# FFN-in products of eleven pairs of steps by seven block products for eight, with two of four weight sums made by transfers that add in place

## The chip, the cores and the metric

One core of one Trainium2 chip runs the kernel. The metric is the device time of one execution in microseconds (us); the median of 3 runs before the change is 1057.72 us (1057.66 to 1057.72). One more execution was recorded by the hardware profiler. The engines are named as in the profile: PE (TensorE, the matmuls), PEld (its weight loads), DVE (VectorE), ACT (ScalarE), POOL (GpSimd), SP (SyncE, which only issues transfers).

## The reference

A decoder trunk of two layers on 256 tokens of width 1024, in float32. Each layer is four blocks, each with a norm ahead and a norm behind it; the FFN blocks, with D_FF = 2816, are what the change touches:

```
def swiglu(x, w_in, w_out):
    gate, up = jnp.split(x @ w_in, 2, axis=-1)
    return (jax.nn.silu(gate) * up) @ w_out
...
        h = swiglu(rms_norm(x, g[0]), w_ffn_in[layer, 0], w_ffn_out[layer, 0])
        x = x + 0.5 * rms_norm(h, g[1])
        h = mixer(rms_norm(x, g[2]))      # layer 0: mLSTM, layer 1: differential attention
        x = x + rms_norm(h, g[3])
        h = swiglu(rms_norm(x, g[4]), w_ffn_in[layer, 1], w_ffn_out[layer, 1])
        x = x + 0.5 * rms_norm(h, g[5])
        x = x + rms_norm((p[layer] @ w_ple) * sigmoid(rms_norm(x, g[6]) @ w_gate), g[7])
```

(The body of a layer is given in outline.) So there are four FFNs, two in each layer; the keys and values that the attention reads are projected once, between the layers.

## The kernel before, in words

Every float32 product of the large layers is three products of split numbers. A number is split into a high half (rounded to the format that TensorE takes at full rate) and a low half (the rest); `mm3` adds hi x hi, hi x lo and lo x hi into one PSUM bank. All weights stream from HBM once, as tiles of 1 MB (128 x 2048), through `weight`: SP loads the tile into a slot `wraw`, ScalarE copies it into `whi` (this rounds it), VectorE writes `wlo` = raw - high. There are 3 slots of raw weights and 5 each of `whi` and `wlo`.

The hidden width of an FFN is cut into 11 steps (`NJ`) of 256 columns, the tokens into two tiles `t` of 128. The function `ffn` has for a step j:

- `stage_in(j, t)`: the FFN-in block. Two weight tiles (the two halves of the width of x), 512 columns each: 256 of gate and 256 of up. `in_block` issues 24 matmuls of 128x512 into a PSUM bank `accI` (8 pieces of x, three products each). ScalarE then makes `sg` = silu(gate), VectorE `h` = up x `sg`, TensorE transposes `h` by two matmuls into the bank `tr`, and the transposed `h` is split into `hh` and `hl`.
- `stage_out(j, t)`: the FFN-out block, one weight tile and 12 matmuls for each token tile into `accO`, which sums over the 11 steps.

The loop runs j from 2 on: both `stage_in` of step j, then both `stage_out` of step j - 1. Steps 0, 1 and 10 are written apart, with the norm at the end (`end`: `post`, then `epilogue`, which makes the next block's transposed input).

The order of instructions is not that of this code. Every call goes to a recorder (`Notes`), which keeps the operations with their dependences and a cost for each. A planner (`play`) then puts them in order for each engine as a list scheduler does: by these costs, urgent ones first, the slots of a ring (such as `wraw`) given out in turn as their last users end. Weight loads and splits are recorded as not urgent. The program is issued in that order, so all instructions have one line in the profile, L363 (L371 after the change), and only the names of tiles tell them apart. A DMA queue's instruction waits in that order too: before the change all transfers but a few at the start are issued by SP.

Of the kernel before, what the change touches and what calls it, by code (L numbers as in the profile page):

```python
# [16 lines left out]
P = 128  # L17
D = 1024
# [13 lines left out]
ATT = 8  # L32

# [15 lines left out]
class Notes:  # L49
# [150 lines left out]
    def cost(self, o, outs, ins):  # L200
# [20 lines left out]
        elif o.eng == "vector":  # L221
# [16 lines left out]
    def play(self, margin):  # L238
# [53 lines left out]
        while len(order) < n:  # L292
# [29 lines left out]
            if e == "sync":  # L322
# [20 lines left out]
            for u in o.users:  # L343
                u.left -= 1
                if u.after[o]:
                    u.ready = max(u.ready, o.end if u.eng != e or e == "sync" else clock[e])
# [19 lines left out]
def trunk(nc, a):  # L366
# [9 lines left out]
    def acc_in():  # L376
        return PT("accI", 512)

    def trp():
        return PT("tr", 512)  # L380
# [21 lines left out]

    def weight(src, n=1, m=1, between=None):
        raw = T([P, 2048], "wraw", 3)
        hi = T([P, 2048], "whi", 5, F32R)
        lo = T([P, 2048], "wlo", 5, F32R)
# [56 lines left out]
    mask_a = T([P, 384], "mask_a", 1)  # L465
    nc.gpsimd.memset(mask_a, 0.0)
    for c0 in (0, 256):
        nc.gpsimd.affine_select(
            out=mask_a[:, c0:c0 + P], in_=mask_a[:, c0:c0 + P], compare_op=ALU.is_ge, fill=BIG,
            base=0, pattern=[[1, P]], channel_multiplier=-1,  # L470
        )

# [41 lines left out]
    def post(t, srcs, gbc, coef):  # L514
        hg = T([P, D], "hg", 3)
# [7 lines left out]
    def new_xt():  # L523
        return T([P, KD, P], "xh", 3, F32R), T([P, KD, P], "xl", 3, F32R)


    def transpose4(src, q):
        pt = trp()
# [15 lines left out]
    def gained(xt, pv, gi, q, into=None):  # L544
# [3 lines left out]
        split(xt[0][:, c, :], xt[1][:, c, :], xg)  # L548

# [11 lines left out]
    def pre(gi, rs, kept=None, raws=None):  # L561
        def go(t):
            xt = new_xt()
            for b in (kept, raws):
                if b is not None:
                    b.append(T([P, KD, P], "mix", 6))
            for q in (0, 4):
                pv = transpose4(x[t], q)
                gained(xt, pv, gi, q, kept and kept[t])
# [8 lines left out]
    def ffn(l, f, xts, rs, epilogue, first=None):  # L578
# [3 lines left out]
        gbc = []  # L582

        def stage_in(j, t):
            if j not in wi:
                wi[j] = in_weights(a["ffn_in"][l, f, j], m=2 if j < 2 or j == NJ - 1 else 1)
            pi = acc_in()
            in_block(pi, xts[t], wi[j])
            sg = T([P, 256], "sg", 3)
            h = T([P, 256], "h", 2)  # L590
            nc.scalar.activation(sg, pi[:, :256], AF.Silu, scale=rs[t])
            nc.vector.scalar_tensor_tensor(h, pi[:, 256:], rs[t], sg, op0=ALU.mult, op1=ALU.mult)
            hh = T([P, 2, P], "hh", 5, F32R)
            hl = T([P, 2, P], "hl", 5, F32R)

# [4 lines left out]
            hT[j, t] = hh, hl  # L600

# [13 lines left out]

        steps = [(0, 0), (0, 1), (1, 0), (1, 1)] if first else [(0, 0), (1, 0), (0, 1), (1, 1)]
# [5 lines left out]
        for j in range(2, NJ - 1):  # L622
            for t in range(NT):
                stage_in(j, t)
            stage_out(j - 1, 0)
            if j < NJ - 2:
                stage_out(j - 1, 1)
        j = NJ - 1
        stage_in(j, 0)
        stage_out(j - 1, 0)  # L630
        stage_out(j - 2, 1)
# [3 lines left out]
        stage_out(j - 1, 1)  # L635
# [8 lines left out]
    def ple(l, xts, rs, epilogue):  # L644
# [3 lines left out]
        php = T([P, 2, 2, S], "whi", 5, F32R)  # L648
# [12 lines left out]
        for t in range(NT):  # L661
            eg = T([P, D], "hg", 3)
            hg = T([P, D], "hg", 3)
# [47 lines left out]
    def mlstm(l, xts, rs, raws, epilogue):  # L711
        qkT = [T([P, HA, S], "mix", 6) for _ in range(2)]
# [8 lines left out]
        sel = T([P, HA, P], "cst", 1)  # L721
        nc.gpsimd.memset(sel, 1.0)
        nc.gpsimd.affine_select(
            out=sel, in_=sel, compare_op=ALU.is_equal, fill=0.0,
            base=0, pattern=[[-1, HA], [0, P]], channel_multiplier=1,
        )
        ones = T([P, S], "sg", 3)
# [463 lines left out]
```

## Time and profile before

| | before |
|---|---|
| median of 3 runs | 1057.72 us |
| the profiled execution | 1057.92 us |
| its span in the trace | 1056.2 us |
| granted TensorE clock, mean | 0.999 |
| PE busy | 1043.5 us (99%) |
| DVE busy | 627.6 us (59%) |
| ACT busy | 546.8 us (52%) |
| POOL busy | 53.8 us (5%) |
| moved by DMA | 191.84 MB, mean 182 GB/s |

The busy times are sums over the whole span, and a matmul's recorded time overlaps that of its neighbours, since matmuls are pipelined: the matmuls named `accI` have a mean duration of 0.39 us, while a run of them proceeds in steps of 0.2271 us. A group's row gives line, engine, operation, the tile written and the tiles read with their shape, then the busy time and the mean of one in ns, then the idle time just before such instructions and what ended it. DVE, ACT and DMA have their load unevenly: high in the FFNs, lower around the mixers.

### The profile page before, as it was taken

What the parts mean: (1) busy time and instruction counts of PE and PEld (TensorE: products, weight loads), DVE (VectorE), ACT (ScalarE), POOL (GpSimd) and SP (SyncE); (2) the same over time, 40 slices, a digit from 0 to 9 for tenths busy, and PEclk for the clock granted to TensorE, in tenths of its full rate; (3) what the DMA queues carried; (4) which work ended last, traced back from release to release, by engine and by line L of the source; (5) the groups of instructions that cost most, each with busy time, mean ns of one, the idle gap of its engine ahead of it and who ended that gap; (6) DMA issues with size and microseconds to landing.
All of it is one profiled execution on the core that took longest, in us unless ns stands there. A gap on an engine that the chain in (4) does not pass through costs nothing.

```text
span 1056.2 us, 12324 instructions
## 1 busy us (share of the span) xinstructions
PE 1043.5 (99%) x4884; PEld 854.5 (81%) x4884; DVE 627.6 (59%) x716; ACT 546.8 (52%) x774; POOL 53.8 (5%) x89
## 2 busy tenths in 40 slices
PE   8999999999999999999999999999999999999997
PEld 6888888887888888888888888888878888888886
DVE  6754453765666454555887454545885855454475
ACT  6644343655556444345776344444676654444363
POOL 1000000100010000000120000000101100000010
PEclk9999999999999999999999999999999999999999
DMA  9854544454256554542647645543435465454521
GB/s 323 307 208 165 210 177 165 180 199 156 87 198 230 177 199 163 205 176 95 219 173 265 224 166 193 198 161 120 179 134 186 150 239 189 170 199 160 199 80 40
DMA packets 29731, 191.84 MB, mean 182 GB/s; under 512 B 3689, under 2 KB 4073, under 8 KB 7657
## 3 DMA queue, kind: packets, MB, share of 16 engines
q1 hardware_dynamic: 29672, 191.06, 51.0%
q8 instruction: 38, 0.62, 0.2%
q14 instruction: 21, 0.16, 0.0%
HBM read 189.99 MB, written 1.05 MB: 181 GB/s over the span
## 4 chain that ended last, share of the span: by engine, by line
PE 91%; DVE 3%; DMA 3%; ACT 1%; SPq 1%; issue 0%; POOL 0%; DVEq 0%; POOLq 0%; ACTq 0%
PE accI L363 59%; PE accO L363 28%; PE tr L363 5%; DMA wraw<-in_ffn_in 1%; DMA wg<-in_mlstm_gates 1%; ACT att L363 1%; DVE att L363 1%; SPq L363 1%; DMA wraw<-in_w_kv 0%; DVE sm L363 0%; POOL sm L363 0%; DVE xl_2r L363 0%; DVE wlo_3r L363 0%; DVE wlo_0r L363 0%; DVE wlo_1r L363 0%
## 5 line engine op out<-in xcount | busy, mean ns | idle before, releaser
L363 ACT ACTIVATE sg<-accI,sm 128x256 f32<-128x256 f32 x88 | 41.7, 474 | 168.6 <-PE accI L363 168.4
L363 DVE SCALAR_TENSOR_TENSOR h<-accI,sm,sg 128x256 f32<-128x256 f32 x88 | 42.4, 481 | 81.8 <-ACT sg L363 81.5
L363 ACT ACTIVATE whi_1r<-wraw 128x1024 fp32r<-128x1024 f32 (+2 forms) x51 | 69.2, 1375 | 30.8 <-PE accO L363 18.1
L363 ACT ACTIVATE whi_3r<-wraw 128x2048 fp32r<-128x2048 f32 (+1 forms) x46 | 68.6, 1505 | 31.1 <-PE accO L363 16.3
L363 ACT ACTIVATE whi_0r<-wraw 128x2048 fp32r<-128x2048 f32 (+2 forms) x47 | 69.1, 1476 | 28.7 <-PE accO L363 14.7
L363 ACT ACTIVATE whi_4r<-wraw 128x1024 fp32r<-128x1024 f32 (+1 forms) x50 | 68.8, 1398 | 26.0 <-PE accO L363 16.0
L363 ACT ACTIVATE whi_2r<-wraw 128x1024 fp32r<-128x1024 f32 (+1 forms) x46 | 67.1, 1467 | 23.7 <-PE accO L363 14.8
L363 POOL TENSOR_SCALAR sm<-sm 128x1 f32<-128x1 f32 x32 | 22.4, 698 | 703.4 <-ACT waste L363 703.4
L363 DVE TENSOR_TENSOR wlo_3r<-wraw,whi_3r 128x2048 fp32r<-128x2048 f32 (+1 forms) x21 | 37.2, 1781 | 27.0 <-ACT whi_3r L363 27.0
L363 DVE TENSOR_TENSOR wlo_1r<-wraw,whi_2r 128x2048 fp32r<-128x2048 f32 (+1 forms) x22 | 39.6, 1805 | 22.2 <-ACT whi_2r L363 22.0
L363 DVE TENSOR_TENSOR wlo_3r<-wraw,whi_4r 128x1024 fp32r<-128x1024 f32 (+1 forms) x27 | 42.3, 1576 | 17.0 <-ACT whi_4r L363 17.0
L363 DVE TENSOR_TENSOR wlo_4r<-wraw,whi_0r 128x2048 fp32r<-128x2048 f32 (+1 forms) x22 | 39.4, 1804 | 21.3 <-ACT whi_0r L363 21.3
L363 DVE TENSOR_TENSOR wlo_2r<-wraw,whi_3r 128x2048 fp32r<-128x2048 f32 (+1 forms) x23 | 41.7, 1825 | 17.3 <-ACT whi_3r L363 17.3
L363 DVE TENSOR_TENSOR wlo_0r<-wraw,whi_0r 128x2048 fp32r<-128x2048 f32 (+2 forms) x23 | 39.8, 1734 | 20.1 <-ACT whi_0r L363 20.0
L363 DVE TENSOR_TENSOR wlo_1r<-wraw,whi_1r 128x2048 fp32r<-128x2048 f32 (+2 forms) x25 | 39.9, 1605 | 17.3 <-ACT whi_1r L363 17.3
L363 DVE TENSOR_TENSOR wlo_0r<-wraw,whi_1r 128x1024 fp32r<-128x1024 f32 (+1 forms) x24 | 39.9, 1665 | 16.1 <-ACT whi_1r L363 16.1
L363 DVE TENSOR_TENSOR wlo_4r<-wraw,whi_4r 128x2048 fp32r<-128x2048 f32 (+1 forms) x21 | 37.3, 1782 | 18.1 <-ACT whi_4r L363 17.8
L363 DVE TENSOR_TENSOR wlo_2r<-wraw,whi_2r 128x1024 fp32r<-128x1024 f32 (+1 forms) x22 | 37.3, 1706 | 16.8 <-ACT whi_2r L363 16.8
L363 PE MATMUL accI<-whi_0r,xh_0r 128*128 128x512 f32 x92 | 36.1, 396 | 0.8 <-ACT whi_0r L363 0.8
L363 PE MATMUL accI<-wlo_0r,xh_0r 128*128 128x512 f32 x92 | 36.0, 394 | 0.5 <-DVE wlo_0r L363 0.5
L363 PE MATMUL accI<-wlo_1r,xh_0r 128*128 128x512 f32 x92 | 36.3, 395 | 0.0
L363 PE MATMUL accI<-whi_3r,xh_0r 128*128 128x512 f32 x92 | 36.2, 393 | 0.0
(439 smaller groups left out, 2824.1 us busy)
## 6 DMA issues: line engine op xcount, KB each, us to landing
wraw<-in_ffn_in SPq DMA_DIRECT2D x86, 1024.0 KB, 4.8
wraw<-in_ffn_out SPq DMA_DIRECT2D x44, 1024.0 KB, 4.8
wraw<-in_mlstm_in SPq DMA_DIRECT2D x12, 1024.0 KB, 4.8
wraw<-in_ple_gate SPq DMA_DIRECT2D x8, 1024.0 KB, 4.8
wraw<-in_w_kv SPq DMA_DIRECT2D x8, 1024.0 KB, 4.8
gbc<-in_norm_g SPq DMA_DIRECT2D x8, 512.0 KB, 6.1
wraw<-in_mlstm_out SPq DMA_DIRECT2D x4, 1024.0 KB, 4.7
wraw<-in_diff_q SPq DMA_DIRECT2D x4, 1024.0 KB, 4.7
```

Source lines behind the costliest of these rows:

```text
L363: getattr(getattr(self.nc, eng), name)(*args, **kw)
```

## The change

In each FFN some pairs of neighbouring steps (j, j + 1) are taken together by a new function, `stage_pair`. `PAIRS` names the first steps: 5 and 8 in the first FFN, 2, 5 and 8 in each of the other three, eleven pairs in all. For a pair the product is seen as 2 x 2 blocks: two token tiles by two halves of x's width, times two halves of the width by two steps. The scheme used is Strassen's in the form with seven products (`times`, 12 matmuls each) in place of eight. What comes with it:

- four combined forms of x (`forms`, once in an FFN: sums and differences of the quarters a11, a12, a21, a22, each split again), kept for all pairs of that FFN;
- seven split weights in place of four: the blocks b11, b21, b22 as loaded, and four sums. Two of these (`t3`, `u1`) are made by transfers: SP loads one block into a slot, and GpSimd's queue issues a second transfer of the other block into the same slot with `accum_op=ALU.add`. The other two (`wt2`, `wt4`) are made by VectorE in place in the slot of b11 or b21;
- seven sums of results of 128x512 on VectorE (`total`), and one copy out of PSUM on ScalarE (`p1`). They lie in the ring `att`, from which `hidden` (the second half of the old `stage_in`) reads.

A pair has seven weight transfers in place of four: five loads by SP, into five slots, and two adding transfers into two of the same slots.

Rings change size: `wraw` 3 to 7 slots, `xh` and `xl` 3 to 4, `accI` in PSUM 2 to 3 banks, `tr` 2 to 1, `hh` and `hl` 5 to 3, `hg` and `sg` 3 to 2. The long-lived tiles `mix` of the mixers are now halves of `wraw` slots (function `pair`), so that fewer of the seven are free while they live; five are free through the FFN that opens layer 1. A few constants of the mixers are smaller or lie elsewhere. The planner counts a GpSimd transfer as 1100 ns of issue and a landing at 200 bytes per ns, against 400 for SP's.

```diff
+NRAW = 7
+NPART = 5
+NX = 4
+NH = 3
+PAIRS = ((5, 8), (2, 5, 8), (2, 5, 8), (2, 5, 8))
...
+        elif o.name == "dma_start" and o.eng == "gpsimd":
+            o.dur, o.lat = 1100, math.prod(c for s, c in outs[0].ap) * 4 / 200.0
...
-        return PT("accI", 512)
+        return PT("accI", 512, 3)
     def trp():
-        return PT("tr", 512)
+        return PT("tr", 512, 1)
...
+    def pair(*shape):
+        b = T([P, 2, *shape], "wraw", NRAW)
+        return [b[:, i] for i in range(2)]
...
+                pv = transpose4(x[t], q, acc_in() if q else None)
+                xg = gained(xt, pv, gi, q, kept and kept[t])
+                if xfs is not None:
+                    xfs.append(xg)
...
+            hidden(j, t, pi)
+        def forms():
+            a11, a12, a21, a22 = xfs
+            s1 = T([P, 4, P], "att", ATT)
+            f1, f2 = new_xt(), new_xt()
+            nc.is_urgent = False
+            for out, x0, x1, op, f_, q in (
+                    (s1, a21, a22, ALU.subtract, f1, 0), (a21, a11, a21, ALU.subtract, f2, 0),
+                    (a11, s1, a11, ALU.subtract, f1, 4), (a12, a12, a11, ALU.add, f2, 4)):
+                nc.vector.tensor_tensor(out, x0, x1, op=op)
+                c = slice(q, q + 4)
+                split(f_[0][:, c, :], f_[1][:, c, :], out)
+            nc.is_urgent = True
+            return [(f[0][:, c, :], f[1][:, c, :]) for f in (f1, f2) for c in (slice(0, 4), slice(4, 8))]
+        def stage_pair(j, j2):
+            if not xf:
+                xf.extend(forms())
+            s1, s2, s3, n4 = xf
+            def load(src, plus=None):
+                raw = T([P, 2048], "wraw", NRAW)
+                nc.sync.dma_start(raw, src)
+                if plus is not None:
+                    nc.gpsimd.dma_start(raw, plus, accum_op=ALU.add)
+                return raw
+            def parts(raw):
+                p_ = part()
+                split(*p_, raw)
+                return p_
+            def add(out, v0, v1):
+                nc.vector.tensor_tensor(out, v0, v1, op=ALU.add)
+                return parts(out)
+            nc.is_urgent = False
+            b11 = load(win[j, 0])
+            t3 = load(win[j2, 0], win[j2, 1])
+            u1 = load(win[j, 0], win[j2, 0])
+            w11 = parts(b11)
+            wt2 = add(b11, b11, t3)
+            b21 = load(win[j, 1])
+            w21 = parts(b21)
+            wu1 = parts(u1)
+            wt3 = parts(t3)
+            b22 = load(win[j2, 1])
+            w22 = parts(b22)
+            wt4 = add(b21, b21, b11)
+            nc.is_urgent = True
+            def times(x_, w):
+                acc_ = acc_in()
+                for kk in range(4):
+                    c = slice(kk * 512, (kk + 1) * 512)
+                    mm3([acc_], x_[0][:, kk, :], x_[1][:, kk, :], [w[0][:, c]], [w[1][:, c]], kk == 0, kk == 3)
+                return acc_
+            def quarter(t, q):
+                return xts[t][0][:, q:q + 4, :], xts[t][1][:, q:q + 4, :]
+            def total(v0, v1, op, out=None):
+                if out is None:
+                    out = piece()
+                nc.vector.tensor_tensor(out, v0, v1, op=op)
+                return out
+            m1 = times(quarter(0, 0), w11)
+            p1 = piece()
+            nc.scalar.activation(p1, m1, AF.Copy)
+            u2 = total(times(s2, wt2), p1, ALU.add)
+            hidden(j, 0, total(times(quarter(0, 4), w21), p1, ALU.add, p1))
+            z = total(times(s1, wu1), u2, ALU.subtract)
+            m3 = times(s3, wt3)
+            total(m3, u2, ALU.add, u2)
+            hidden(j2, 1, total(z, m3, ALU.subtract))
+            hidden(j2, 0, total(times(n4, w22), z, ALU.add, z))
+            hidden(j, 1, total(times(quarter(1, 4), wt4), u2, ALU.add, u2))
...
+        last = (1,)
+        j = 2
+        while j < NJ - 1:
+            item = (j, j + 1) if j in PAIRS[2 * l + f] else (j,)
+            if len(item) == 2:
+                stage_pair(*item)
+            else:
+                for t in range(NT):
+                    stage_in(j, t)
+            j += len(item)
+            for i in last:
+                stage_out(i, 0)
+            if j < NJ - 1:
+                for i in last:
+                    stage_out(i, 1)
+                left = ()
+            else:
+                left = last
+            last = item
...
+    xfs = [xT[t][:, c, :] for t in range(NT) for c in (slice(0, 4), slice(4, 8))]
+    xts = ffn(0, 0, xts, rs, xfs, pre(1, rq, kept), first)
+    rs, xfs = [], []
+    xts = mlstm(0, xts, rq, kept, pre(2, rs, xfs=xfs))
     rq = []
-    xts = ffn(0, 1, xts, rs, pre(3, rq))
+    xts = ffn(0, 1, xts, rs, xfs, pre(3, rq))
```

How the rows move. In the rows below `wraw_71` to `wraw_77` are slots of raw weights (71 to 73 before), `whi_0r` to `whi_4r` and `wlo_0r` to `wlo_4r` the five split buffers each, `accI_92` and up PSUM banks, `att_100` and up the ring that holds the forms of x and the results, `hl_0r` and up the low half of the transposed `h`.

VectorE in the middle of the second FFN, before:

```order
L363 TENSOR_TENSOR wlo_4r<-wraw_73,whi_4r 128x2048
L363 SCALAR_TENSOR_TENSOR h_113<-accI_94,sm_9_184,sg_126 128x256
L363 TENSOR_TENSOR wlo_0r<-wraw_71,whi_0r 128x2048
L363 TENSOR_TENSOR hl_3r<-tr_100,hh_3r 128x256
L363 TENSOR_TENSOR wlo_1r<-wraw_72,whi_1r 128x2048
L363 SCALAR_TENSOR_TENSOR h_114<-accI_93,sm_5_180,sg_125 128x256
L363 TENSOR_TENSOR hl_0r<-tr_99,hh_0r 128x256
```

The same engine in a pair of that FFN, after:

```order
L371 TENSOR_TENSOR wraw_73<-wraw_73,wraw_72 128x2048
L371 SCALAR_TENSOR_TENSOR h_109<-accI_93,sm_9_172,sg_116 128x256
L371 TENSOR_TENSOR hl_1r<-tr_99,hh_1r 128x256
L371 TENSOR_TENSOR wlo_4r<-wraw_71,whi_4r 128x2048
L371 TENSOR_TENSOR hl_2r<-tr_99,hh_2r 128x256
L371 TENSOR_TENSOR wlo_3r<-wraw_73,whi_3r 128x2048
L371 TENSOR_TENSOR hl_1r<-tr_99,hh_1r 128x256
L371 TENSOR_TENSOR wraw_71<-wraw_71,wraw_73 128x2048
L371 TENSOR_TENSOR wlo_0r<-wraw_74,whi_0r 128x2048
L371 TENSOR_TENSOR wlo_1r<-wraw_72,whi_1r 128x2048
L371 TENSOR_TENSOR att_105<-accI_92,att_103 128x512
```

Where splits of weights alternated with the work on `h`, two weight sums (wraw from wraw) and the first sum of results stand among them, and a split now waits behind a sum; the first row waits for the adding transfer into `wraw_72`.

VectorE behind step 1 of the second FFN, before (the first splits of steps 2 and 3):

```order
L363 SCALAR_TENSOR_TENSOR h_113<-accI_94,sm_5_180,sg_127 128x256
L363 TENSOR_TENSOR hl_2r<-tr_100,hh_2r 128x256
L363 TENSOR_TENSOR wlo_4r<-wraw_71,whi_4r 128x2048
L363 SCALAR_TENSOR_TENSOR h_114<-accI_93,sm_9_184,sg_126 128x256
L363 TENSOR_TENSOR wlo_0r<-wraw_72,whi_0r 128x2048
L363 TENSOR_TENSOR hl_0r<-tr_99,hh_0r 128x256
```

And after, where the first pair follows:

```order
L371 TENSOR_TENSOR att_103<-att_105,att_107 128x512
L371 TENSOR_TENSOR att_105<-att_104,att_105 128x512
L371 TENSOR_TENSOR hl_0r<-tr_99,hh_0r 128x256
L371 TENSOR_TENSOR att_104<-att_103,att_104 128x512
L371 TENSOR_TENSOR xl_0r<-att_103,xh_0r 128x512
L371 TENSOR_TENSOR xl_1r<-att_105,xh_1r 128x512
L371 TENSOR_TENSOR att_100<-att_100,att_104 128x512
L371 SCALAR_TENSOR_TENSOR h_108<-accI_92,sm_9_172,sg_117 128x256
L371 TENSOR_TENSOR wlo_0r<-wraw_73,whi_0r 128x2048
L371 TENSOR_TENSOR hl_1r<-tr_99,hh_1r 128x256
```

The four forms of x (att from att) and their splits (`xl_0r`, `xl_1r`) have come in ahead of the splits of weights.

VectorE at the second pair of the third FFN, after, from the last read of slot `wraw_75` to the sum that needs the weight that was loaded and added there:

```order
L371 TENSOR_TENSOR wlo_4r<-wraw_75,whi_0r 128x2048
L371 TENSOR_TENSOR hl_1r<-tr_99,hh_1r 128x256
L371 SCALAR_TENSOR_TENSOR h_109<-att_107,sm_1_164,sg_116 128x256
L371 TENSOR_TENSOR wlo_0r<-wraw_73,whi_1r 128x2048
L371 TENSOR_TENSOR hl_2r<-tr_99,hh_2r 128x256
L371 TENSOR_TENSOR wlo_1r<-wraw_72,whi_2r 128x2048
L371 TENSOR_TENSOR wlo_2r<-wraw_74,whi_3r 128x2048
L371 TENSOR_TENSOR wlo_3r<-wraw_77,whi_4r 128x2048
L371 SCALAR_TENSOR_TENSOR h_108<-accI_92,sm_10_173,sg_117 128x256
L371 TENSOR_TENSOR wraw_77<-wraw_77,wraw_75 128x2048
```

Between the two reads of `wraw_75` stand four splits of weights, two `h` and two `hl`; in that time a load by SP and an adding transfer have to land in it.

GpSimd's queue ahead of the second FFN (the norms' small operations `sm`), before and after:

```order
L363 TENSOR_TENSOR sm_15_152<-sm_14_151,mhalf_136 128x4
L363 TENSOR_TENSOR sm_2_139<-sm_1_138,mhalf_136 128x4
L363 TENSOR_SCALAR sm_1_176<-sm_4_141 128x1
L363 TENSOR_TENSOR sm_3_178<-sm_1_176,mhalf_136 128x1
L363 TENSOR_SCALAR sm_2_177<-sm_5_142 128x1
```

```order
L371 TENSOR_TENSOR sm_2_127<-sm_1_126,mhalf_124 128x4
L371 DMA wraw_75<-in_ffn_in 128x2048
L371 DMA wraw_76<-in_ffn_in 128x2048
L371 TENSOR_SCALAR sm_1_164<-sm_4_129 128x1
L371 TENSOR_TENSOR sm_3_166<-sm_1_164,mhalf_124 128x1
```

Two adding transfers of the second FFN's first pair have moved in ahead of the norm that closes the mLSTM block.

More of the change, by code (lines that the diff above doesn't have):

```diff
@@ L345, in play @@
                 if u.after[o]:
-                    u.ready = max(u.ready, o.end if u.eng != e or e == "sync" else clock[e])
+                    u.ready = max(u.ready, o.end if u.eng != e or o.name == "dma_start" else clock[e])
                     if u.eng != e:
@@ L634, in ffn @@
         stage_in(j, 1)
-        stage_out(j - 1, 1)
+        for i in last:
+            stage_out(i, 1)
         stage_out(j, 1)
@@ L711, in mlstm @@
     def mlstm(l, xts, rs, raws, epilogue):
-        qkT = [T([P, HA, S], "mix", 6) for _ in range(2)]
+        qkT = pair(HA, S)
         qT, kT = qkT
@@ L891, in shared_k @@
     def shared_k(xts, rs):
-        kT = [T([P, 4, S], "mix", 6) for _ in range(2)]
+        kT = pair(4, S)
         ws = [in_weights(a["w_kv"][b], m=2) for b in range(2)]
@@ L924, in diff_attn @@
         lam_init = 0.8 - 0.6 * math.exp(-0.3 * l)
-        qT = [T([P, 4, S], "mix", 6) for _ in range(2)]
+        qT = pair(4, S)
         ws = [in_weights(a["diff_q"][b]) for b in range(2)]
```

138 lines of the change are left out of this document (64 added, 74 removed).

## The prediction

> **What bounds the kernel now.** I read the page's busy line first, then TensorE's own waits, then the chain of waits, then busy time by stage. The columns of the busy line are engine, us, share and instructions; those of the waits are us in total, times, longest.
>
> ```profile
> span 1056.2 us, 12324 instructions
> PE 1043.5 (99%) x4884; PEld 854.5 (81%) x4884; DVE 627.6 (59%) x716; ACT 546.8 (52%) x774; POOL 53.8 (5%) x89
> ...
> PE tr L363 <- DVE h L363: 1.3, 2, 1.1
> PE accI L363 <- ACT xh_0r L363: 1.1, 1, 1.1
> ```
>
> TensorE is idle for 12.7 us of 1056.2, and its longest waits are about 1 us. Its share could still be hollow, so I look at the spacing in the chain of waits (start, us, what) and at two FFN middles by stage (engine columns as in the answer's heading: PE, PEld, DVE, ACT, POOL, granted clock, DMA share, GB/s).
>
> ```profile
> 57.21 7.04 PE accI L363 x31
> 74.17 7.04 PE accI L363 x31
> ...
> core 0: us, PE busy (x) PEld busy (x) DVE busy (x) ACT busy (x) POOL busy (x), PEclk, DMA share, GB/s
> 57.21:159.03 101.82, 101.82 (x457) 83.33 (x457) 51.38 (x44) 45.34 (x44) 0.00 (x0) 1.00 0.53 186
> 357.56:476.35 118.79, 118.79 (x533) 97.21 (x533) 59.90 (x52) 51.94 (x52) 0.00 (x0) 1.00 0.53 186
> ```
>
> 31 matmuls in 7.04 us are 0.2271 us each, at the full granted clock. One FFN step j (48 FFN-in and 24 FFN-out matmuls, 4 transposes) repeats every 74.17 - 57.21 = 16.96 us. Six such steps are the 101.82 us of the second fence: TensorE never stops, VectorE is busy 51.38 us (8.56 a step, 50%), ScalarE 45%, DMA 53%. So a matmul taken away here is worth its whole 0.227 us until something else fills up; what counts is how near VectorE and DMA come.
>
> The prices (us in total, then mean ns of one; the last rows are a stretch of VectorE's timeline, start and us):
>
> ```profile
> L363 ACT ACTIVATE whi_0r<-wraw 128x2048 fp32r<-128x2048 f32 x25 | 47.9, 1917 | 21.1 <-PE accO L363 13.3 <-PE accI L363 6.8 <-DMA wraw<-in_ffn_in 1.0
> L363 ACT ACTIVATE sg<-accI,sm 128x256 f32<-128x256 f32 x88 | 41.7, 474 | 168.6 <-PE accI L363 168.4
> L363 ACT ACTIVATE att<-tr 128x512 f32<-128x512 f32 x6 | 3.6, 595 | 2.6 <-PE tr L363 2.1 <-DVE sm L363 0.5
> L363 ACT ACTIVATE hh_0r<-tr 128x256 fp32r<-128x256 f32 x18 | 6.9, 383 | 16.3 <-PE tr L363 16.3
> L363 DVE TENSOR_TENSOR wlo_0r<-wraw,whi_0r 128x2048 fp32r<-128x2048 f32 x13 | 29.8, 2292 | 17.5 <-ACT whi_0r L363 17.5
> L363 DVE TENSOR_TENSOR wlo_0r<-wraw,whi_0r 128x1024 fp32r<-128x1024 f32 x6 | 7.2, 1221 | 0.7 <-ACT whi_0r L363 0.6
> L363 DVE TENSOR_TENSOR hg<-accO,gbc 128x512 f32<-128x512 f32 x22 | 14.2, 686 | 14.3 <-PE accO L363 14.3
> L363 DVE SCALAR_TENSOR_TENSOR h<-accI,sm,sg 128x256 f32<-128x256 f32 x88 | 42.4, 481 | 81.8 <-ACT sg L363 81.5
> L363 DVE TENSOR_TENSOR hl_1r<-tr,hh_1r 128x256 fp32r<-128x256 f32 x18 | 7.6, 423 | 11.1 <-ACT hh_1r L363 11.0
> ...
> 196.10 2.29 DVE L363 TENSOR_TENSOR wlo_4r<-wraw,whi_4r 128x2048 fp32r<-128x2048 f32 x1
> 198.30 0.42 DVE L363 TENSOR_TENSOR hl_1r<-tr,hh_1r 128x256 fp32r<-128x256 f32 x1
> 198.63 2.28 DVE L363 TENSOR_TENSOR wlo_0r<-wraw,whi_0r 128x2048 fp32r<-128x2048 f32 x1
> ```
>
> In the stretch each instruction starts 0.09 us before the last one's recorded end, so a full VectorE advances 0.09 us faster per instruction than its durations say.
>
> **Part 1: matmuls removed.** A pair of steps had 96 FFN-in matmuls and now has 7 products of 12, so 84. Eleven pairs: 132 x 0.2271 = 30.0 us off the path. The built order agrees, 4746 matmul rows before and 4614 after. A pair now takes TensorE 2 x 16.96 - 2.73 = 31.2 us.
>
> **Part 2: VectorE in a pair.** Two old steps were 17.1 us. Added: 3 weight splits (7 for 4) at 2.29 = 6.9; 2 weight sums of 128x2048, which no row shows with a plain f32 result, priced as the split of that shape, 4.6; 7 result sums of 128x512 at 0.69 = 4.8. Together 33.4 us by durations, and with 29 instructions x 0.09 of overlap 30.8, against 31.2 of TensorE. So inside a pair VectorE is level with TensorE. A pair and the single step behind it are 33.4 + 8.6 = 42.0 us of 48.2, so a lag can be made up, and five buffers of split weights let VectorE run ahead. Bounds for eleven pairs: 0, and 2.2 us (33.4 - 31.2) each, 24. I take 0, because in the built order the seven products of a later pair stand in one unbroken run and, buffer by buffer, each split has 2 to 4 us to spare: a buffer freed by one product is needed again five products later, 10.9 us, and the refill behind it is 1.92 on ScalarE and 2.29 on VectorE. ScalarE in a pair: 9 splits x 1.92, one copy at 0.6, 4 x 0.47, 4 x 0.38 = 21.3 of 31.2 us, hidden.
>
> **Part 3: the first pair of the last three FFNs** comes straight after steps 0 and 1, and the four combined forms of x have to be made there too (4 sums and 4 splits of 128x512 on VectorE, 8 x 0.69 = 5.5 us, once per FFN). The stretch that it falls into, in the second FFN, from the second half of the norm before it to the end of step 0's output:
>
> ```profile
> 311.37:340.30 28.93, 28.93 (x136) 23.75 (x135) 22.35 (x25) 17.62 (x26) 3.49 (x4) 1.00 0.69 248
> ```
>
> VectorE has 22.35 of 28.93 us. In place of 9.3 us of splits for later steps (3 x 2.29 and 2 x 1.22) it must give the forms (5.5) and two splits, a sum and a split (9.2) until the second product begins at 343.0: 27.8 of 31.6 us, which just fits. From there to the last product, 13.7 us of TensorE, it has 4 splits and a sum (11.5), 5 result sums (3.4), 2 h (1.0), one hl (0.4) and the two halves of the next output split (2.4): 18.7, less 16 x 0.09, is 17.3. That is 3.6 us too much; part of it TensorE covers with output matmuls that need only the high half of the weight. I take 2 us for each of three FFNs, 6 in all; bounds 0 and 3 x 3.6 = 11. The first FFN's first pair stands at step 5 and makes its forms early, at no cost.
>
> **Part 4: the 22 adding transfers.** Nothing in the trace adds while it moves. The nearest rows (KB of each, us to landing), and a stretch in which DMA was nearly full:
>
> ```profile
> wraw<-in_ffn_in SPq DMA_DIRECT2D x86, 1024.0 KB, 4.8
> gbc<-in_norm_g SPq DMA_DIRECT2D x8, 512.0 KB, 6.1
> ...
> 15.00:40.00 25.00, 24.16 (x106) 18.95 (x107) 18.32 (x24) 18.59 (x29) 1.90 (x4) 1.00 0.92 349
> ```
>
> 349 GB/s at a share of 0.92 is 379 GB/s full, so a plain megabyte holds DMA for 2.8 us. An adding one cannot land sooner than the plain 4.8 us; the dearest big transfer, 512 KB in 6.1, would be 12.2 for this size. I take 7.6, the plain landing plus a second pass of 2.8 for reading what stands in SBUF: of the two ends it is nearer to the plain row, which has the same shape and the same source. Load of a pair and a single step: 10 plain and 2 adding transfers, 28 + 11 = 39 of 48.2 us; in the pair alone 7 and 2, 31 of 31.2. Tight, but a slot waits ahead. The slots: between the last read of a slot and the sum that needs the added weight there, the built order has at least 10.2 us of VectorE work (second pair of the third FFN, where only five slots of raw weights are free; 10.7 for the pair after it, 14 to 31 elsewhere). Load and add need 4.8 + 7.6 = 12.4 there, so VectorE waits some 2 us at two pairs, with the h and hl of the single step queued behind the sum; the second product needs the split of that sum about 4 us later, so TensorE does not see it. Cost 0; bounds 0 and, with 12.2 us a transfer, 2 x 3 = 6. On GpSimd they stand ahead of norms: at the second FFN two of them ahead of the norm behind mLSTM's output, and each waits for its plain load. That load's slot is freed before that norm's sums begin and lands within the 4.6 us for which TensorE still has the second half of that projection, so I cost it at nothing. SP's queue gives 33 more loads, each 0.33 us to issue, hidden.
>
> What a busy VectorE does to GpSimd, whose instruction now issues transfers:
>
> ```profile
> 202.74 2.28 DVE L363 TENSOR_TENSOR wlo_1r<-wraw,whi_1r 128x2048 fp32r<-128x2048 f32 x1
> ...
> 203.10 2.08 POOL L363 TENSOR_SCALAR sm<-sm 128x1 f32<-128x1 f32 x1 [8.19 <-ACT waste L363]
> 208.19 0.30 POOL L363 TENSOR_SCALAR sm<-sm 128x1 f32<-128x1 f32 x1 [2.36 <-ACT waste L363]
> ```
>
> The same instruction took 0.30 us alone and 2.08 under a split: it ended with it. Carried over to an adding transfer, it starts up to 2 us late, which the 4 us above absorb. The Trainium skill (SBUF — State Buffer, "SBUF: two separate sides") has a rule against this change: descriptors of a transfer issued from GpSimd cannot be written while VectorE holds the shared port in a two-port mode, so the transfer stands still; an instruction with two SBUF inputs, by the same section, shuts out only a GpSimd operation that reads SBUF. By its first half each transfer here would stall and the sum would be that of the starving rival below; by its second half the sum stays. The row agrees with the second half for an instruction that reads SBUF, and shows nothing for a transfer.
>
> **Part 5: smaller rings** (transposes' PSUM 2 to 1, hh and hl 5 to 3, hg 3 to 2, and long-lived tiles moved into the raw-weight slots). 176 FFN transposes now wait for the last one's hl, but two stand about 5.5 us apart and the read-out is 0.38 + 0.42. 0 to 4 us, mostly at the stage borders; I take 1.
>
> **Sum.** The profiled execution took 1057.9 (span 1056.2 and 1.7 around it), 0.2 above the median of 1057.7. 1057.9 - 30.0 + 0 + 6 + 0 + 1 = 1034.9, so 1035.
>
> **Rivals.** (A) Everything is hidden: parts 3 and 5 cost nothing, 1057.7 - 30 = 1028. For it, TensorE's 12.7 us of idle time in all of before; against it, the 3.6 us of part 3. (B) VectorE is the bound in every pair: 1.5 us of the 2.2 on average, 16 us more, 1051. For it, 33.4 against 31.2 us in a fixed order, where a wait for TensorE is not made good; against it, the overlap and the single steps. (C) Slower: an adding transfer holds DMA so long that DMA is the bound. It binds from (48.2 - 28)/2 = 10.1 us each and the gain is gone at (50.9 - 28)/2 = 11.5, four plain ones. At the 12.2 of the gbc row a pair and a step take 28 + 24.4 = 52.4, 1.5 more than before: 11 x 1.5 + 7, 1081. For it, no row excludes it; against it, a second read is one more pass, not four. (D) Transfers starve behind VectorE, which only pauses when it stands at the sum and waits: 7.6 us less the 4 of cover, 11 times, 1035 + 40 = 1075. For it, the 2.08 us row; against it, that the row ends with one instruction. That the matmuls are not saved is excluded by the built order.
>
> **Chances.** 1030 to 1042 as summed: 0.56. A: 0.13. B, 1042 to 1058: 0.18. C: 0.10. D: 0.03. 0.2% of the time, 2.1 us, is about what a measurement of this kernel tells from no change. B's far end gives same 0.03 and a little of slower; faster 0.85, slower 0.12. The range leaves out C, D and B's last part: 1027 to 1055.
>
> **What would show it.** Right: 11 x 12 fewer matmuls of accI, still 0.227 apart; VectorE near 98% in a pair, TensorE idle only in the first pairs. Part 4 right: an adding transfer lands in under 10 us, and no big wait of VectorE for DMA at wraw<-wraw. B would show as TensorE waiting for wlo in every pair; C as a DMA share near 1 through the FFNs and ScalarE and VectorE waiting for wraw; D as GpSimd's transfer instructions lasting many us. A granted clock under 1.00 would spoil all of it.

## The result, and the profile after

The changed kernel takes 1048.87 us (median; 1046.08 to 1050.41) against 1057.72: ratio 0.9912, 95% interval 0.9888 to 0.9936. It is faster, by 8.9 us where 22.7 were forecast. The spread of 4.3 us is larger than before (0.7), and the slower of these runs have the lower mean clock: 1050.41 at 0.990, 1046.08 at 0.995. The profiled execution took 1050.06, its span is 1048.3.

| | before | after |
|---|---|---|
| median | 1057.72 us | 1048.87 us |
| span of the profiled execution | 1056.2 us | 1048.3 us |
| TensorE busy, idle (span less busy) | 1043.5, 12.7 us | 1017.8, 30.5 us |
| granted clock, mean | 0.999 | 0.992 |
| landing of a 1 MB load of `ffn_in` from SP / of an adding transfer (median) | 4.8 us / none | 5.7 us / 13.0 us |

The page's busy line, the line of GpSimd's queue (packets, MB, share of the 16 DMA engines over the span) and the row of the adding transfers:

```profile
span 1048.3 us, 12394 instructions
PE 1017.8 (97%) x4752; PEld 832.0 (79%) x4752; DVE 806.6 (77%) x880; ACT 617.4 (59%) x835; POOL 73.6 (7%) x108
...
q0 software_dynamic: 3168, 23.07, 11.0%
...
wraw<-in_ffn_in POOLq DMA_DIRECT2D x22, 1024.0 KB, 13.0
```

The 132 matmuls are gone (4884 to 4752), 30 us. The span fell by only 7.9, because TensorE's idle time grew by 17.8 us and its busy time fell by 25.7, not 30. What it waits for, and what VectorE waits for (us in total, times, longest):

```profile
PE tr L371 <- DVE hl_1r L371: 5.2, 2, 4.1
PE tr L371 <- DVE hl_0r L371: 3.7, 1, 3.7
...
PE tr L371 <- DVE hl_2r L371: 2.0, 1, 2.0
```

```profile
DVE wraw L371 <- DMA wraw<-in_ffn_in: 21.7, 4, 7.6
```

The big waits of TensorE are for the low half of a transposed h, which stands on VectorE behind a weight sum, and VectorE stood at that sum: four times, 21.7 us. One of the four, the second pair of the third FFN, in the chain of waits (start, us), and then on the timelines of GpSimd and VectorE (start, us, in brackets the idle time before):

```profile
592.29 4.73 DMA wraw<-in_ffn_in
597.66 12.37 DMA wraw<-in_ffn_in
```

```profile
597.66 0.87 POOL L371 DMA_DIRECT2D wraw<-in_ffn_in  x1 [48.44 <-DMA wraw<-in_ffn_in]
600.61 0.86 POOL L371 DMA_DIRECT2D wraw<-in_ffn_in  x1 [2.08 <-DMA wraw<-in_ffn_in]
...
602.04 0.48 DVE L371 SCALAR_TENSOR_TENSOR h<-accI,sm,sg 128x256 f32<-128x256 f32 x1
610.13 2.29 DVE L371 TENSOR_TENSOR wraw<-wraw,wraw 128x2048 f32<-128x2048 f32 x1 [7.61 <-DMA wraw<-in_ffn_in]
```

The slot came free at 592.2, its plain load took 4.73 us, the adding transfer 12.37, and VectorE, done with its other work at 602.5, waited until 610.1 (17.8 us from the free slot to the landing, against 10.3 us of work). The same stretch by windows of 2 us, and behind it a stretch of the fourth FFN (columns: PE, PEld, DVE, ACT, POOL, granted clock, DMA share, GB/s):

```profile
598.00:600.00 2.00, 2.00 (x10) 1.66 (x9) 2.00 (x2) 0.00 (x0) 0.53 (x1) 1.00 1.02 406
606.00:608.00 2.00, 2.00 (x11) 1.65 (x9) 0.00 (x0) 0.47 (x1) 0.00 (x0) 1.00 0.98 270
...
610.00:612.00 2.00, 0.00 (x0) 0.00 (x0) 1.87 (x1) 0.00 (x0) 0.00 (x0) 1.00 1.04 234
...
614.00:616.00 2.00, 2.00 (x8) 1.58 (x7) 1.60 (x1) 2.00 (x2) 0.00 (x0) 0.66 0.44 90
616.00:618.00 2.00, 2.00 (x6) 1.56 (x5) 2.00 (x3) 0.44 (x2) 0.00 (x0) 0.50 0.00 0
...
900.00:902.00 2.00, 1.27 (x6) 1.03 (x7) 2.00 (x3) 1.90 (x1) 0.00 (x0) 0.84 0.99 274
902.00:904.00 2.00, 2.00 (x6) 1.61 (x5) 0.87 (x1) 0.38 (x1) 0.00 (x0) 0.50 1.00 283
```

DMA is full from 598 to 614, at 406 GB/s from 598 to 600, while plain loads run, and at 213 to 320 in the windows from 602 to 614. TensorE stops for 3.7 us (to 613.2), and from 616 to 618 it does 6 matmuls in 2 us where it did 10 or 11: its granted clock is 0.50. Over the four places the stops are 1.0, 3.7, 4.1 and 2.0 us, together 10.9; the clock lost at the last three (in windows of 2 us, 1 less the granted clock, times 2) is 1.7, 3.4 and 1.7 us, together 6.8. Some 0.7 us of the 3.4 falls into its own stop (the clock is low from 665.8, TensorE starts again at 667.2), so 6.1 us come on top. That is 17.0 us, against 18.4 that the first experiment below finds for the adding transfers; where the rest lies is not shown.

Where TensorE stood in the stop of 3.7 us, when VectorE split the sum that had been late, and when the second product, the first that needs this split, began:

```profile
613.20 0.44 PE L371 MATMUL tr<-ident,h 128*128 128x128 f32 x2 [3.68 <-DVE hl_0r L371]
...
614.40 2.29 DVE L371 TENSOR_TENSOR wlo_4r<-wraw,whi_0r 128x2048 fp32r<-128x2048 f32 x1 [1.26 <-ACT whi_0r L371]
...
625.59 0.39 PE L371 MATMUL accI<-whi_0r,xh_2r 128*128 128x512 f32 x1
```

TensorE did not wait for the sum's split, which was done 8.9 us before the second product began. It waited ahead of the whole pair, for the work on `h` that stood behind the sum on VectorE.

### The profile page after: what moved, and what is told of

Same layout as the page of the kernel before. It is cut to its first block, busy times and chain, and to the rows that moved or that the text cites. A ratio compares the mean times of both kernels' runs of the same rounds, so it can differ in the third digit from the quotient of the medians.

```text
span 1048.3 us, 12394 instructions
## 1 busy us (share of the span) xinstructions
PE 1017.8 (97%) x4752; PEld 832.0 (79%) x4752; DVE 806.6 (77%) x880; ACT 617.4 (59%) x835; POOL 73.6 (7%) x108
## 4 chain that ended last, share of the span: by engine, by line
PE 85%; DMA 8%; DVE 3%; ACT 2%; issue 1%; POOL 0%; SPq 0%; POOLq 0%; DVEq 0%; ACTq 0%
PE accI L371 55%; PE accO L371 26%; DMA wraw<-in_ffn_in 7%; PE tr L371 4%; DMA x<-in_x 1%; DVE att L371 1%; DMA wraw<-in_diff_out 0%; ACT att L371 0%; DVE wlo_1r L371 0%; DVE wraw L371 0%; POOL sm L371 0%; DVE h L371 0%; DVE sm L371 0%; ACT whi_4r L371 0%; SPq L371 0%
## 5 line engine op out<-in xcount | busy, mean ns | idle before, releaser
L371 ACT ACTIVATE whi_2r<-wraw 128x2048 fp32r<-128x2048 f32 (+1 forms) x54 | 80.3, 1499 | 26.6 <-DVE wraw L371 8.0
L371 ACT ACTIVATE whi_1r<-wraw 128x2048 fp32r<-128x2048 f32 (+2 forms) x53 | 81.9, 1555 | 18.0 <-PE accI L371 8.1
L371 ACT ACTIVATE whi_3r<-wraw 128x1024 fp32r<-128x1024 f32 (+1 forms) x56 | 80.4, 1451 | 15.4 <-PE accI L371 5.1
L371 ACT ACTIVATE whi_4r<-wraw 128x1024 fp32r<-128x1024 f32 (+1 forms) x55 | 79.8, 1472 | 12.2 <-PE accI L371 7.0
L371 ACT ACTIVATE sg<-accI,sm 128x256 f32<-128x256 f32 x44 | 20.8, 473 | 85.3 <-PE accI L371 84.9
L371 DVE TENSOR_TENSOR wraw<-wraw,wraw 128x2048 f32<-128x2048 f32 x22 | 50.2, 2283 | 21.7 <-DMA wraw<-in_ffn_in 21.7
L371 DVE TENSOR_TENSOR att<-accI,att 128x512 f32<-128x512 f32 x66 | 45.3, 686 | 20.1 <-PE accI L371 20.0
L371 DVE TENSOR_TENSOR wlo_2r<-wraw,whi_3r 128x1024 fp32r<-128x1024 f32 (+1 forms) x29 | 48.7, 1695 | 4.2 <-ACT whi_3r L371 4.2
L371 DVE TENSOR_TENSOR wlo_0r<-wraw,whi_1r 128x2048 fp32r<-128x2048 f32 (+1 forms) x25 | 48.4, 1943 | 0.3 <-ACT whi_1r L371 0.3
L371 PE MATMUL tr<-ident,h 128*128 128x128 f32 x176 | 34.7, 279 | 11.5 <-DVE hl_1r L371 5.2
L371 PEld LDWEIGHTS tr<-ident,h 128*128 128x128 f32 x176 | 23.5, 141 | 26.4 <-DVE hl_1r L371 6.0
```

What stands on the lines that cost most here:

```text
L371: getattr(getattr(self.nc, eng), name)(*args, **kw)
```

## The experiments

Theory T: the adding transfers land too late at four pairs, VectorE waits, TensorE stops, and each longer stop brings a low clock behind it. The rivals were that VectorE is too full in a pair, that the smaller rings cost the time, or that it is the second transfer as such, not the adding.

**e1: the plain load alone in the slots of t3 and u1.**

```diff
-                if plus is not None:
-                    nc.gpsimd.dma_start(raw, plus, accum_op=ALU.add)
```

> The 22 adding transfers are left out: the slots of t3 and u1 get their plain load alone (so the two sums miss one block each), all else as in the changed kernel. Theory T (the adding transfers land too late, VectorE waits for them at four pairs, TensorE stops there for 10.9 us and its granted clock stays low for some microseconds after each stop, 6.8 us worth): 1048.9 - 17 = 1032, range 1030 to 1035, no wait of VectorE for wraw at a weight sum, clock 0.998 or more. Rival V (VectorE is too full in a pair, the transfers only show where it is late anyway): 1043 or more.

Measured: 1030.47 us (1030.31 to 1031.58), ratio 0.9745 (0.9730 to 0.9759), clock 0.999. So the adding transfers cost 18.4 us, and everything else together 2.8 (1057.7 - 30 = 1027.7). In the stretches of the two worst stops TensorE now never stops, with VectorE at four fifths:

```profile
590.00:620.00 30.00, 30.00 (x136) 24.53 (x135) 24.27 (x17) 14.75 (x14) 0.00 (x0) 1.00 0.51 197
640.00:670.00 30.00, 30.00 (x136) 24.68 (x135) 23.19 (x17) 15.12 (x13) 0.00 (x0) 1.00 0.51 193
```

**e2: the second transfer overwrites.** Only `accum_op` is taken away; all engines keep their order.

```diff
-                    nc.gpsimd.dma_start(raw, plus, accum_op=ALU.add)
+                    nc.gpsimd.dma_start(raw, plus)
```

> The second transfer into the slots of t3 and u1 stays on GpSimd's queue with the same waits, but overwrites instead of adding (so the two sums miss one block each). The order of all engines is that of the changed kernel. Theory T with the DMA time of an adding megabyte (5.2 us against 2.7) as its cause: a landing of 5 to 8 us, at most short waits of VectorE, 1033 to 1038. Rival S (it is the second transfer as such, from GpSimd's queue behind the first load, that is late): landings over 10 us and 1044 or more.

Measured: 1032.74 us (1032.59 to 1034.18), ratio 0.9767 (0.9752 to 0.9781). The queue's line and the landing:

```profile
q0 software_dynamic: 3168, 23.07, 5.6%
...
wraw<-in_ffn_in POOLq DMA_DIRECT2D x22, 1024.0 KB, 8.3
```

With the same packets, the share is 5.6% of 1031.0 us, 2.6 us of all DMA engines for a megabyte; adding takes 11.0% of 1048.3, 5.2 us. VectorE still waits, 6.5 us in three places, and TensorE hardly sees it. The time is 0.3 us under the range of T and the landing, 8.3, a little over it, but short of the rival's 10. The second transfer as such costs 2.3 us of the 18.4; the adding costs the rest.

**e3: the rings without the pairs.**

```diff
-PAIRS = ((5, 8), (2, 5, 8), (2, 5, 8), (2, 5, 8))
+PAIRS = ((), (), (), ())
```

> No pairs at all, but the changed rings, mixers and masks of the changed kernel. Theory R (the smaller rings and the slots shared with the mixers cost 4.9 us of TensorE's idle time in differential attention, and a step is 0.13 us shorter, 44 x 0.13 = 5.7): 1057.7 + 4.9 - 5.7 = 1057, range 1053 to 1061, with some 6 us of TensorE idle in the attention. Rival (the attention suffers only from the pairs' early weights of the FFN behind it): idle there 1.4 us as before, 1052.

Measured: 1057.67 us (1055.71 to 1058.52), ratio 0.9997 (0.9987 to 1.0006): no difference, out of two opposed ones. The stretch of differential attention, before and in e3 (from one norm's end to the other):

```profile
743.20:832.27 89.07, 87.65 (x508) 72.19 (x507) 67.95 (x109) 62.90 (x160) 10.98 (x14) 1.00 0.42 148
```

```profile
736.17:832.08 95.91, 90.67 (x517) 73.63 (x516) 69.98 (x110) 63.48 (x161) 10.66 (x14) 1.00 0.50 176
```

It takes 6.8 us longer (3.8 more of it idle), in the changed kernel 97.4 us. It had started 7.0 us earlier: an FFN step takes 16.83 us in place of 16.96, since its two runs of 12 accO matmuls take 2.72 and 2.75 us, not 2.80 and 2.78. Which ring does this I did not try.

**e4: the planner told that an adding transfer lands after 13.1 us.**

```diff
-            o.dur, o.lat = 1100, math.prod(c for s, c in outs[0].ap) * 4 / 200.0
+            o.dur, o.lat = 1100, math.prod(c for s, c in outs[0].ap) * 4 / 80.0
```

> The planner is told that an adding transfer lands 13.1 us after its start (80 bytes per ns in place of 200), nothing else. Theory T: the planner puts other work of VectorE ahead of the sums that wait, so part of the four waits goes: 1038 to 1046. Rival (the slots come free too late whatever the order, since the load itself waits for its slot): 1047 to 1051.

Measured: 1068.03 us (1065.87 to 1068.95), ratio 1.0100 (1.0083 to 1.0117). Both theories missed: it is slower than before. No wait of VectorE for an adding transfer is left, but its timeline in the third pair of the second FFN shows why that did not help:

```profile
431.10 0.42 DVE L371 TENSOR_TENSOR hl_0r<-tr,hh_0r 128x256 fp32r<-128x256 f32 x1 [2.67 <-PE accO L371]
431.44 2.28 DVE L371 TENSOR_TENSOR wraw<-wraw,wraw 128x2048 f32<-128x2048 f32 x1
435.70 2.29 DVE L371 TENSOR_TENSOR wlo_3r<-wraw,whi_3r 128x2048 fp32r<-128x2048 f32 x1 [1.98 <-ACT whi_3r L371]
437.90 2.28 DVE L371 TENSOR_TENSOR wraw<-wraw,wraw 128x2048 f32<-128x2048 f32 x1
440.11 2.29 DVE L371 TENSOR_TENSOR wlo_1r<-wraw,whi_1r 128x2048 fp32r<-128x2048 f32 x1
442.31 2.28 DVE L371 TENSOR_TENSOR wlo_4r<-wraw,whi_4r 128x2048 fp32r<-128x2048 f32 x1
```

The sum now stands behind an hl that waits for TensorE; VectorE idles ahead of it, and then all splits of the pair are due at once, while TensorE is busy for 5.55 us of 10:

```profile
440.00:450.00 10.00, 5.55 (x18) 3.97 (x19) 9.65 (x7) 5.97 (x5) 0.00 (x0) 0.83 0.88 341
```

A landing that the planner expects late delays all that depends on it in a fixed order, whether the transfer is late there or not. That this is the whole of the 19 us is argued from one place and not shown.

**e5: the transfers by themselves.** The trunk is replaced by transfers of 1 MB with VectorE operations between them. Two of its loops, an adding transfer alone, and two adding ones with three plain ones behind:

```diff
+    for n in range(3):
+        plus(r0, 1 + n)
+        sync((r0,))
...
+        plus(r1, 1 + n)
+        plus(r0, 4 + n)
+        for k, r in enumerate((r2, r3, r4)):
+            nc.sync.dma_start(r, win[6 + k, n % 2])
```

> Only transfers of 1 MB and VectorE operations that order them; the trunk is left out. Three times each: an adding transfer alone, a plain one from GpSimd's queue alone, a plain one from SP alone, two adding ones freed 2.2 us apart, two adding ones with three plain loads of SP behind them, an adding one under five VectorE sums. Theory C (company: the DMA time of an adding megabyte, 5.2 us, is shared among those in flight): alone 7 to 8 us, two at once 10 to 12, with the plain loads 13 or more, under VectorE as alone. Rival A (the adding itself is slow to land, whatever is beside it): alone already 11 to 13. Rival D (VectorE holds it back): under the sums 4 us or more longer than alone.

Issue on GpSimd and the first use on VectorE, from the timeline: alone, overwriting alone, two adding, two adding with three plain loads behind:

```profile
38.39 0.87 POOL L371 DMA_DIRECT2D ra<-in_ffn_in  x1 [14.63 <-DVE ra L371]
46.36 2.29 DVE L371 TENSOR_TENSOR ra<-ra,one 128x2048 f32<-128x2048 f32 x1 [8.28 <-DMA ra<-in_ffn_in]
...
81.55 0.54 POOL L371 DMA_DIRECT2D ra<-in_ffn_in  x1 [11.96 <-DVE ra L371]
86.54 2.29 DVE L371 TENSOR_TENSOR ra<-ra,one 128x2048 f32<-128x2048 f32 x1 [5.35 <-DMA ra<-in_ffn_in]
...
198.02 0.86 POOL L371 DMA_DIRECT2D ra<-in_ffn_in  x1 [17.11 <-DVE ra L371]
200.23 0.86 POOL L371 DMA_DIRECT2D rb<-in_ffn_in  x1 [1.34 <-DVE rb L371]
205.92 2.29 DVE L371 TENSOR_TENSOR ra<-ra,one 128x2048 f32<-128x2048 f32 x1 [6.09 <-DMA ra<-in_ffn_in]
211.61 2.29 DVE L371 TENSOR_TENSOR rb<-rb,one 128x2048 f32<-128x2048 f32 x1 [3.41 <-DMA rb<-in_ffn_in]
...
298.37 0.88 POOL L371 DMA_DIRECT2D ra<-in_ffn_in  x1 [1.32 <-DVE ra L371]
312.50 2.29 DVE L371 TENSOR_TENSOR ra<-ra,one 128x2048 f32<-128x2048 f32 x1 [5.27 <-DMA ra<-in_ffn_in]
```

8.0 us alone (46.36 - 38.39), 5.0 without adding; two at once 7.9 and 11.4; with plain loads the second takes 14.1 (13.5 in the two other repeats), and the plain loads behind land after 12 to 12.6 us. Under a run of VectorE sums DMA was done with an adding transfer 7.4 us after its issue (at 328.65; alone, issued at 38.39, it was done before 46), no later than alone:

```profile
335.00:336.00 1.00, 1.00 (x1) 0.00 (x0) 1.00 0.76 156
336.00:337.00 1.00, 1.00 (x1) 0.00 (x0) 1.00 0.01 0
```

So company makes the landing late, and these sums of VectorE do not hold it back.

**e6: u1 by VectorE in all pairs, t3 by transfer.**

```diff
-            u1 = load(win[j, 0], win[j2, 0])
+            u1 = load(win[j2, 0])
...
             w11 = parts(b11)
+            nc.vector.tensor_tensor(u1, u1, b11, op=ALU.add)
```

> In all eleven pairs u1 is summed by VectorE (in the slot of a plain load, 2.29 us more of VectorE in a pair), only t3 arrives by an adding transfer. Theory C: one adding transfer in flight lands in 8 to 9 us, no long waits; VectorE has 35 us of work for 31.2 of TensorE in a pair, some of it shows: 1036, range 1032 to 1043. Rival V (VectorE is the bound of a pair, 2.3 us more come through): 1030.5 + 11 x 2 = 1052.

Measured: 1044.59 us (1042.18 to 1046.60), ratio 0.9876 (0.9857 to 0.9896). The number lies between the two, over the range of C: one adding transfer among plain loads still lands in 11.8 us, where 8 to 9 were expected, so it needs no second one beside it to be late, and VectorE still waits for it (us in total, times, longest):

```profile
DVE wraw L371 <- DMA wraw<-in_ffn_in: 12.8, 5, 5.1
```

**e7: both sums by VectorE, at the four late pairs only.** Here `late` holds for these four; the other seven keep their adding transfers.

```diff
+            late = (2 * l + f, j) in ((1, 5), (2, 5), (2, 8), (3, 5))
+            t3 = load(win[j2, 0], None if late else win[j2, 1])
+            u1 = load(win[j2, 0]) if late else load(win[j, 0], win[j2, 0])
+            t3b = load(win[j2, 1]) if late else None
...
+            if late:
+                nc.vector.tensor_tensor(t3, t3, t3b, op=ALU.add)
+                nc.vector.tensor_tensor(u1, u1, b11, op=ALU.add)
```

> At the four pairs where VectorE waited for an adding transfer (second pair of the second FFN, second and third of the third, second of the fourth) both sums are made by VectorE from plain loads; the other seven pairs keep their adding transfers. Theory T: the four waits and the stops behind them go, 17 us; VectorE's 4.6 us more at each of four pairs cost 0 to 2 us each: 1036, range 1031 to 1042. Rival V: 1045 or more.

Measured: 1032.88 us (1032.41 to 1033.95), ratio 0.9769 (0.9753 to 0.9786), 16 us under the changed kernel and 24.8 under the one before. The remaining 14 adding transfers land little sooner (11.9 us against 13.0), and no wait of VectorE for them is left:

```profile
PE 1010.9 (98%) x4752; PEld 827.3 (80%) x4752; DVE 823.6 (80%) x888; ACT 616.4 (60%) x835; POOL 66.8 (6%) x100
...
wraw<-in_ffn_in POOLq DMA_DIRECT2D x14, 1024.0 KB, 11.9
```

**e8: the third FFN with its first pair only.** `PAIRS = ((5, 8), (2, 5, 8), (2,), (2, 5, 8))`.

> The third FFN keeps its first pair only. Theory T: two pairs less saved (+5.5 us), their two waits gone with the 7.8 us of idle TensorE and the 5.1 us of low clock behind them: 1048.9 + 5.5 - 12.9 = 1041.5, range 1038 to 1045: fewer pairs are faster. Rival (the waits only move to the next pair): 1050 or more.

Measured: 1044.31 us (1043.87 to 1045.57), ratio 0.9877 (0.9862 to 0.9891). Two pairs fewer are faster, by 4.6 us where 7.4 were expected. The other two late pairs still wait, the longer one 5.7 us:

```profile
DVE wraw L371 <- DMA wraw<-in_ffn_in: 8.3, 2, 5.7
```

**e9: VectorE held by its own work in place of the transfers.** As e1, with 1, 3, 3 and 2 passes ahead of the sum at the four places, which the planner counts as 1 ns each.

```diff
+            for _ in range({(1, 5): 1, (2, 5): 3, (2, 8): 3, (3, 5): 2}.get((2 * l + f, j), 0)):
+                nc.vector.tensor_tensor(t3, t3, t3, op=ALU.max)
             wt2 = add(b11, b11, t3)
```

> As the run with the plain loads alone (no adding transfers), but at the four pairs where VectorE had waited, VectorE does 1, 3, 3 and 2 idle passes (maximum of a tile with itself, 2.29 us each, 20.6 us in all against 21.7 us waited) right ahead of the weight sum; their cost is hidden from the planner, so the order stays. Theory T (the time goes by VectorE's lateness at these four places, and a TensorE stop of 2 us or more brings a low clock behind it whatever made it): 10 us of TensorE idle and 5 to 7 us by the clock, 1030.5 + 16 = 1046, range 1042 to 1049, clock 0.991 to 0.995. Rival K (the low clock comes with the adding transfers' traffic, not with the stop): clock 0.998 or more, 1040. Rival M (the transfers cost elsewhere, by the shared DMA): 1036 or less.

Measured: 1049.52 us (1049.18 to 1050.88), ratio 0.9925 (0.9910 to 0.9940), clock 0.991: all of the loss is back, with no adding transfer in the program. By windows, with almost no DMA traffic:

```profile
608.00:610.00 2.00, 0.00 (x0) 0.00 (x0) 1.10 (x2) 1.26 (x1) 0.00 (x0) 0.86 0.00 0
610.00:612.00 2.00, 0.57 (x3) 0.57 (x4) 1.05 (x2) 2.00 (x3) 0.00 (x0) 0.50 0.00 0
612.00:614.00 2.00, 2.00 (x6) 1.58 (x6) 1.57 (x1) 0.72 (x1) 0.00 (x0) 0.50 0.04 8
614.00:616.00 2.00, 2.00 (x6) 1.56 (x5) 0.36 (x2) 0.38 (x1) 0.00 (x0) 0.50 0.00 0
```

So the low clock follows the stop, not the traffic, and VectorE's lateness at these places is enough for a loss of this size. That it is the same size is in part chance: TensorE stops at three of the four places here, for 4.7, 6.0 and 2.5 us, together 13.2 against 10.9 in the changed kernel.

**e10: both sums by VectorE in all eleven pairs**, the edit of e7 without `late`.

> No adding transfer at all: in all eleven pairs t3 and u1 are summed by VectorE from plain loads (4.6 us more of VectorE in a pair, 38 us against 31.2 of TensorE; one load more). If VectorE, level with TensorE inside a pair, can make up in the single steps behind (pair and step: 46.6 against 48.2 us): 1033, range 1030 to 1037, as fast as the mixed version. Rival V (VectorE is now the bound, 2 us or more come through at each pair): 1050 or more.

Measured: 1040.13 us (1038.93 to 1041.63), ratio 0.9839 (0.9822 to 0.9855). Between the two: VectorE, with 38 us of work in a pair against 31.2, shows by 9.7 us over e1, 0.9 a pair. A whole program without adding transfers beats the change by 8.7 us; adding transfers where they have time beat both.

**e11: e7 without the first pairs of the last three FFNs.** `PAIRS = ((5, 8), (5, 8), (5, 8), (5, 8))`.

> The mixed version without the first pair of the last three FFNs (pairs at 5 and 8 only, eight in all). It loses 3 x 2.73 = 8.2 us of saved matmuls and gains what a first pair costs. My price of 2 us each: 1032.9 + 8.2 - 6 = 1035. If a first pair costs next to nothing: 1040 to 1041.

Measured: 1038.48 us (1038.24 to 1038.91), ratio 0.9819 (0.9804 to 0.9833). Three pairs fewer cost 5.6 us, 1.9 a pair, so a first pair pays 1.9 of its 2.73; its price is 0.9 us.

## Why the prediction was right or wrong

The direction was right, the size was wrong: 8.9 us, not 22.7. The step that failed is part 4, the adding transfers. That the range, 1027 to 1055, holds the time is luck: part 4 at its far bound gives 1041, and the stretch from 1042 on stood for rival B, which did not come. Parts 3 and 5 were some 4 us too dear together, which hid as much of part 4's miss.

- **Part 1, right.** 132 matmuls fewer, still 0.227 apart wherever TensorE runs, 30 us; e1 reaches 1030.5.
- **Part 2, right, cost 0.** e1, with the same work on VectorE, leaves 2.8 us for everything; e10 shows that the margin is thin: 4.6 us more in each pair cost 0.9.
- **Part 3, too dear.** Taken as 6 us, measured by e11 as 3 x 0.86 = 2.6, nearly all of the 2.8 that e1 leaves.
- **Part 4, the failed step: "Cost 0", with 6 as its far bound; measured 18.4** (e1 against the change). What held: the slack at the second pair of the third FFN, 10.2 us taken, was 10.3, VectorE's work from 592.2 to 602.5. The adding transfer by itself, 7.6 taken, lands in 8.0 (e5). Its second pass of DMA time is there, 5.2 us against 2.6 (e2). Two things failed. The first is the landing in company. I let a transfer land as if DMA were its own, though the same part said that a pair fills DMA to 31 of 31.2 us; the adding transfers and the loads beside them share it, and it took 12.4 there, 13.0 in the median. So there were four waits and not two. The second is the path to TensorE. I had the second product as the place where TensorE needs what VectorE is late with, about 4 us on, "so TensorE does not see it". It stood earlier, at the transposes, for the h and hl that I had put behind the sum myself. Some 4 us were covered at that pair all the same (a wait of 7.6 gave a stop of 3.7), by the matmuls that TensorE still had ahead of those transposes; that the number fits is luck. At the three other places waits of 7.1, 4.2 and 2.8 us gave stops of 4.1, 2.0 and 1.0, so that some 3, 2 and 2 us were covered.
- **Its far bound failed too.** At 12.2 us a transfer I had 3 us of stop at two pairs. That nearly came out (3.7 and 4.1), but the other two, for which I had 14 us of slack or more, stopped as well (1.0 and 2.0), and no term held the low clock behind a stop, 6.1 us. I named a granted clock under 1.00 as a thing that would spoil the sum, and gave it no price.
- **Part 5, right in sum.** Taken as 1, measured 0 (e3), out of 6.8 us lost in the attention and as much gained in the steps. SP's queue has 11 loads of `ffn_in` more (97 against 86), not the 33 that part 4 names; 22 of those 33 are GpSimd's, and no cost hung on it.
- **The rivals.** B, VectorE as the bound, fell with e1 and e7. C, DMA as the bound throughout, did not come: an adding megabyte holds DMA for 5.2 us, under the 10.1 from which it binds. D, starving behind VectorE, is refuted by e5 for sums such as these. The rule of the Trainium skill on the shared port (SBUF — State Buffer, "SBUF: two separate sides") agrees by its second half: sums of two SBUF inputs did not hold the adding transfer. What its first half says no run here tests.

The double DMA time of an adding transfer agrees with the Trainium skill (Collectives: The Full Stack, "The bandwidth ceiling: the fold count and why AG ≠ RS ≠ AR"), where the add of a ReduceScatter reads two sources and so has half the rate of an AllGather, which copies; e2 and the change give 2.6 and 5.2 us.

## What to carry to other kernels

Price a transfer's landing with what moves beside it, and compare load plus transfer with the work that stands between two uses of its slot: where that work is shorter, the engine that uses the slot waits for the whole difference. Then follow its queue: all that stands behind the wait is late too, and another engine may need that first. Use an adding transfer where its slot waits long, and sum on the compute engine where it does not; neither everywhere was best (1032.9 against 1048.9 and 1040.1). Where a stop of TensorE of some 2 us is possible, add the low clock behind it, which here was 0.6 of the stops again (6.1 of 10.9 us).

## What the runs showed of the hardware that I had not expected

- An adding transfer of 1 MB takes the DMA engines 5.2 us against 2.6 for a plain one on the same queue, and lands alone in 8.0 us against 5.0. Plain loads that are in flight with two of them land in 12 to 12.6 us, not 4.8.
- After a stop of TensorE of 1.0 us the clock stayed at 1.00; after stops of 2.0 and 3.7 us it was 0.50 for 3.4 us, and at the stop of 4.1 us for 6.8 us, 1.3 of them within the stop (the clock lost, 1.7, 1.7 and 3.4, over one half). The Trainium skill (TensorE: Matmul & The Clock Gate, "Part 1: The HAM clock gate") has the clock halved after an idle window of about 3.4 us, and full again after as much of work; the halving agrees, and the low stretch behind the stops of 3.7 and 2.0 us, but a stop of 2.0 us was enough here.
- The time of the changed kernel varied by 4.3 us between runs, lower clock with longer time, that of e7, which has hardly a stop, by 1.5. That the stops make it vary is not shown: e9, with longer stops, varied by 1.7, and e3, without pairs, by 2.8.
